# Holding the gathered rows' products and the weightings of reloaded tiles to TensorE's progress, two halves back

## The chip, the cores and the metric

One core of a Trainium2 chip runs one program. The metric is the device time of one execution in microseconds (us), lower is better. Engines: PE (TensorE, matmuls), DVE (VectorE), ACT (ScalarE), POOL (GpSimd), SP (SyncE, which issues most DMAs). Each works through its own queue in the order in which the program puts it there.

## What is computed

One layer of a two-branch model for 128 prompt tokens and 512 sample tokens: a mixer, then a layer of single-neuron experts (PEER). The change lies in the latter:

```python
s = jnp.einsum('chpd,hpnd->chpn', q, sub_keys)           # scores against 2 x 128 sub-keys per head
top_s, top_pos = lax.top_k(cand, PEER_TOPK)              # 16 experts of 16384 per head, 8 heads
g = jax.nn.softmax(top_s, axis=-1)
ue = jnp.take(peer_u, ids, axis=0)                       # rows of 2048 numbers
act = jax.nn.gelu(jnp.einsum('chkd,cd->chk', ue, xb))
ve = jnp.take(peer_v, ids, axis=0)
return jnp.einsum('chk,chkd->cd', g * act, ve)
```

Then x = LN2(ALPHA * x + gate2 * PEER(u)).

## The kernel before

PEER is computed in two ways at once. The 128 prompt tokens and the first 64 sample tokens are gathered: for each of their chosen experts an indirect DMA on POOL's queue (L825) brings 128 rows of 2048 numbers into a tile `rows`, 192 times from `peer_u` and 192 times from `peer_v`. A row tile of `peer_u` is multiplied by the tokens and summed in one DVE instruction (L858, `ustep`), one of `peer_v` is scaled and added to `gacc` in one (L869, `vstep`). These two are "products" below. There are three buffers for `rows`, four in the last stage.

The other 448 sample tokens go the dense way, through all 16384 experts. In the **S stage** PE computes scores `sps` of all experts, block by block (`s_half`, L934 to L936); ACT turns them into `ge` (L949), which is stored to DRAM (`ge_d`). Beside it a table of gates is built with small matmuls (L1024) and stored as `g_d`. In the **V stage** `ge` is loaded again (L1050) with its part of the table (`gt`, L1043), DVE multiplies them (L1061, the "weighting"), ACT rounds the product (L1063), DVE takes the rest (L1064), and PE multiplies with `peer_v` into `vps` (L88 to L90); DVE adds each `vps` to `vaccT` (L1139). `prep(e, ...)` issues the steps from L1050 to L1064 for expert block e, one block after each pair of halves in the V stage, and the first eight blocks in the S stage's last stretch.

The weights of both stages come 512 KB at a time into `wraw` (L82), which serves one **half**: 24 matmuls in the S stage as in the V stage. Each is split in two: ACT rounds it to `whi` (L76), DVE takes the rest, `wlo` (L77). Every third matmul of a half needs `wlo`. `wraw` has three buffers, and `whi` and `wlo` have three each as well, so the split for a half can be made only when PE has finished the half three before.

After each half the program notes its last matmul in `marks` and calls `pace`, which lets the gathers go on by `R_A` = 0.8 steps (by `r_v` in the V stage). One step of `gather_gen` issues a gather and, when as many are on the way as there are buffers, also the product of the oldest. The gather itself is tied to PE: `after(d, LAG)` makes it wait for the mark `LAG` = 2 halves back. `after` is this:

```python
def after(d, lag):
    if len(marks) > lag:
        tc.add_manual_dep(d.ins, marks[-1 - lag].ins.name, ...)
```

The order in each engine's queue is not the order in which the program is written: the framework that builds the program places instructions by its own estimate of when each can run, as far as their dependencies let it. A dependency on a mark is thus two things, a wait on the chip and a bound on how early the instruction can be placed.

Of the kernel before, what the change touches and what calls it, by code (L numbers as in the profile page):

```python
# [12 lines left out]
ALU = mybir.AluOpType  # L13
# [21 lines left out]
def layer_kernel(ctx: ExitStack, tc: tile.TileContext, i: dict, y_p: bass.AP, y_s: bass.AP, st_o: bass.AP):  # L35
# [786 lines left out]
    def gather_gen():  # L822
# [32 lines left out]

        def ustep(t, p, r):
            u, _, coef, dots, idx, gt_ = ctxs[t]
            V.scalar_tensor_tensor(r, r, 1.0, u, op0=ALU.mult, op1=ALU.mult, accum_out=dots[:, p:p + 1])  # L858
            if p % NBLK == NBLK - 1:
                sl = slice(p + 1 - NBLK, p + 1)  # L860
                S.activation(coef[:, sl], dots[:, sl], AF.Gelu_apprx_tanh)
                V.tensor_tensor(coef[:, sl], coef[:, sl], gt_[:, sl], op=ALU.mult)

        def vstep(t, p, r):
            _, acc, coef, _, idx, _ = ctxs[t]
            if p == 0:
                V.tensor_scalar(acc, r, coef[:, 0:1], None, op0=ALU.mult)
            else:
                V.scalar_tensor_tensor(acc, r, coef[:, p:p + 1], acc, op0=ALU.mult, op1=ALU.add)  # L869
            if t == 0 and p == 127:  # L870
                yield from close(acc, 0, 0, y_p[0])
            if t == 1 and p == 63:
                up = row_tile("up")
                Q.dma_start(up[0:NG2], acc[NG2:2 * NG2])
                yield
                acc = acc[0:NG2]
                V.tensor_tensor(acc, acc, up[0:NG2], op=ALU.add)
                yield from close(acc, 1, 128, y_s[0, 0:NG2])
# [29 lines left out]
    R_Q, R_A = 0.4, 0.8  # L908
    G_MOD, G_DVE = 4, 1
    gg = gather_gen()  # L910
    LAG = 2
    due, left = [0.0], [2 * (128 + 64) + 12]

    def pace(n):
# [116 lines left out]
    with ExitStack() as es:  # L1031
# [5 lines left out]
        gts_, loads, wts = {}, {}, {}  # L1037
# [14 lines left out]
        def prep(e, buf, x):  # L1052
            load_gt(e // 4)
            load_ge(e)
            if e % 4 == 0:
                load_gt(e // 4 + 1)
            for n in range(1, 4):
                load_ge(e + n)
            ge = loads[e]
            gev = ge.rearrange("p (b t) -> p b t", t=32)  # L1060
            V.tensor_tensor(gev, gev, gts_[e // 4][:, :, e % 4, :], op=ALU.mult)  # L1061
            eh, el = buf[:, x, :], buf[:, 8 + x, :]
            S.copy(eh, ge)  # L1063
            V.tensor_tensor(el, ge, eh.bitcast(F32), op=ALU.subtract)  # L1064
            wts[e] = (eh, el)
# [158 lines left out]
```

## Time and profile before

| what | us |
|---|---|
| three runs | 3967.94, 3979.97 (median), 3989.53 |
| the profiled execution | 3966.88 |
| its span, first to last instruction | 3964.8 |
| PE busy | 3768.2 |
| DVE busy | 3100.9 |
| DVE idle before products until rows landed, 1240 to 3934 us (140.4 + 135.8 + 45.6 + 32.5) | 354.3 |

The gathers and their products begin near 1240 us, the S stage's main stretch is 1470 to 2646 us, the V stage 2646 to 3934 us. Busy time of PE is the union of its matmuls, so what lacks to a stretch's length is time without a matmul. A line of the waits says which engine and line sat idle, until what was done, for how long in total, how often, and the longest. In the timelines the bracket at a row's end is the idle time of the engine just before it and what ended it. An idle engine costs only where PE ends up waiting for it.

### The profile page before, as it was taken

The numbers are of one execution on the slowest core, as the hardware profiler recorded it, in microseconds if no ns is written. First come the engines' busy times: TensorE is split into PE (matmuls) and PEld (weight loads), VectorE is DVE, ScalarE is ACT, GpSimd is POOL, SyncE is SP. The second block draws the span as 40 slices with busy tenths as digits, with TensorE's granted clock in tenths as the row PEclk, the third lists the DMA queues.
The fourth block names the chain that finished last, engine by engine and source line by source line (L and its number), as shares of the span: only waits on it lengthen the run. The fifth ranks groups of instructions, "written<-read, shape, count | busy, mean of one in ns | idle before, by whom it ended". The sixth has DMA issues, their size and how long they took to land.

```text
span 3964.8 us, 53756 instructions
## 1 busy us (share of the span) xinstructions
PE 3768.2 (95%) x20405; PEld 3357.2 (85%) x20405; DVE 3100.9 (78%) x4529; ACT 1595.3 (40%) x2707; POOL 721.1 (18%) x522
## 2 busy tenths in 40 slices
PE   7899899799999999999999999999999999999996
PEld 2688777678879989899898998888988899999896
DVE  5599965657899978788787887567887888888867
ACT  2111354533464347666666666223222222222221
POOL 0000111410000112222212222122222123322200
PEclk8899999999989999999999999999999999999998
DMA  9665444586444668898898898989998899999992
GB/s 363 209 204 179 154 138 163 170 257 233 155 144 166 209 236 303 288 326 319 292 325 292 305 325 290 326 307 334 336 332 322 322 332 329 339 330 347 321 241 80
DMA packets 408882, 1054.87 MB, mean 266 GB/s; under 512 B 27904, under 2 KB 253136, under 8 KB 355424
## 3 DMA queue, kind: packets, MB, share of 16 engines
q1 hardware_dynamic: 353328, 648.76, 49.2%
q0 software_dynamic: 55296, 402.68, 27.4%
q8 instruction: 160, 2.62, 0.3%
q14 instruction: 98, 0.80, 0.1%
HBM read 979.37 MB, written 71.38 MB: 265 GB/s over the span
## 4 chain that ended last, share of the span: by engine, by line
PE 61%; DMA 15%; DVE 13%; issue 6%; ACT 2%; POOL 2%; SPq 0%; DVEq 0%; POOLq 0%; ACTq 0%
PE vps L90 7%; PE vps L88 7%; PE vps L89 7%; PE sps L936 7%; PE sps L934 7%; PE sps L935 7%; DMA wa<-in_w_ada 3%; DVE wlo L77 3%; DMA rows<-in_peer_v,ids 3%; PE adab L156 2%; DMA gt<-g_d 2%; PE mm L258 2%; PE mm L256 2%; PE mm L89 2%; PE mm L90 2%
## 5 line engine op out<-in xcount | busy, mean ns | idle before, releaser
L76 ACT CAST whi<-wraw 128x1024 fp32r<-128x1024 f32 x704 | 737.5, 1049 | 1733.2 <-DMA wraw<-in_peer_v 346.2
L77 DVE TENSOR_TENSOR wlo<-wraw,whi 128x1024 fp32r<-128x1024 f32 x704 | 863.0, 1228 | 171.5 <-ACT whi L76 168.9
L934 PE MATMUL sps<-u2hi_a,whi 128*128 128x448 f32 x1760 | 648.9, 369 | 14.7 <-ACT ge L949 11.7
L936 PE MATMUL sps<-u2hi_a,wlo 128*128 128x448 f32 x1760 | 648.5, 368 | 6.5 <-DVE wlo L77 6.5
L935 PE MATMUL sps<-u2lo_a,whi 128*128 128x448 f32 x1760 | 647.9, 368 | 0.0
L869 DVE SCALAR_TENSOR_TENSOR gacc<-rows,coefs,gacc 128x2048 f32<-128x2048 f32 x190 | 446.3, 2349 | 186.5 <-DMA rows<-in_peer_v,ids 140.4
L858 DVE SCALAR_TENSOR_TENSOR rows<-rows,urow 128x2048 f32<-128x2048 f32 x192 | 439.2, 2288 | 168.7 <-DMA rows<-in_peer_u,ids 135.8
L90 PE MATMUL vps<-ehd,wlo 128*128 128x448 f32 x1024 | 377.3, 368 | 12.2 <-DVE wlo L77 12.2
L90 PE MATMUL vps<-ehl,wlo 128*128 128x448 f32 x1024 | 375.0, 366 | 8.9 <-DVE wlo L77 8.9
L89 PE MATMUL vps<-ehd,whi 128*128 128x448 f32 x1024 | 376.4, 368 | 0.0
L88 PE MATMUL vps<-ehd,whi 128*128 128x448 f32 x1024 | 376.3, 367 | 0.0
L88 PE MATMUL vps<-ehl,whi 128*128 128x448 f32 x1024 | 374.9, 366 | 0.0
L89 PE MATMUL vps<-ehl,whi 128*128 128x448 f32 x1024 | 374.3, 366 | 0.0
L934 PEld LDWEIGHTS sps<-u2hi_a,whi 128*128 128x128 f32 x1760 | 333.4, 189 | 42.9 <-ACT ge L949 12.2
L825 POOL DMA_INDIRECT rows<-in_peer_u,ids x128 | 189.8, 1483 | 983.8 <-PE gps L1024 287.0
L936 PEld LDWEIGHTS sps<-u2hi_a,wlo 128*128 128x128 f32 x1760 | 333.2, 189 | 37.5 <-DVE wlo L77 8.8
L935 PEld LDWEIGHTS sps<-u2lo_a,whi 128*128 128x128 f32 x1760 | 333.4, 189 | 26.9
L825 POOL DMA_INDIRECT rows<-in_peer_v,ids x128 | 193.3, 1510 | 514.8 <-PE gps L1024 140.1
L1020 ACT ACTIVATE A<-ab,gsp,nij 128x128 fp32r<-128x128 f32 x672 | 284.6, 487 | 1.6 <-DVE nij L1001 1.5
L332 DVE SCALAR_TENSOR_TENSOR ybuf<-z,par,ybuf 128x655 f32<-128x655 f32 x240 | 220.6, 921 | 6.4
L90 PEld LDWEIGHTS vps<-ehd,wlo 128*128 128x128 f32 x1024 | 192.9, 188 | 31.7 <-DVE wlo L77 14.5
L90 PEld LDWEIGHTS vps<-ehl,wlo 128*128 128x128 f32 x1024 | 192.2, 188 | 28.5 <-DVE wlo L77 12.5
(301 smaller groups left out, 7073.3 us busy)
## 6 DMA issues: line engine op xcount, KB each, us to landing
wraw<-in_peer_uT SPq DMA_DIRECT2D x256, 512.0 KB, 5.6
wraw<-in_peer_v SPq DMA_DIRECT2D x256, 512.0 KB, 6.1
wa<-in_w_ada SPq DMA_DIRECT2D x192, 512.0 KB, 4.1
wraw<-in_w_in SPq DMA_DIRECT2D x64, 512.0 KB, 4.7
wraw<-in_w_out SPq DMA_DIRECT2D x64, 512.0 KB, 6.0
wraw<-in_w_query SPq DMA_DIRECT2D x64, 512.0 KB, 3.5
ge_d<-ge SPq DMA_DIRECT2D x128, 224.0 KB, 5.2
g_d<-gst SPq DMA_DIRECT2D x14, 2048.0 KB, 13.4
```

The costliest lines, as they stand in the source:

```text
L76: S.copy(hi, raw)
L77: V.tensor_tensor(lo, raw, hi.bitcast(F32), op=ALU.subtract)
L88: T.matmul(out, ah, bh, start=first, stop=False)
L89: T.matmul(out, ah, bl, start=False, stop=False)
L90: return T.matmul(out, al, bh, start=False, stop=last)
L825: d = G.indirect_dma_start(out=r, out_offset=None, in_=src, in_offset=bass.IndirectOffsetOnAxis(ap=idx, axis=0))
L858: V.scalar_tensor_tensor(r, r, 1.0, u, op0=ALU.mult, op1=ALU.mult, accum_out=dots[:, p:p + 1])
L869: V.scalar_tensor_tensor(acc, r, coef[:, p:p + 1], acc, op0=ALU.mult, op1=ALU.add)
L934: T.matmul(sps, wh[:, kk, :], u2hi_a[:, k, :], start=(k == 0), stop=False)
L935: T.matmul(sps, wh[:, kk, :], u2lo_a[:, k, :], start=False, stop=False)
L936: mk = T.matmul(sps, wl[:, kk, :], u2hi_a[:, k, :], start=False, stop=(k == KT - 1))
L1020: S.activation(A[:, x], ab, AF.Relu, scale=nij[:, 1 + x, n:n + 1], bias=gsp[:, x, n:n + 1])
```

## The change

`after` gets a second use. The two products in `ustep` and `vstep` and the weighting in `prep` now also depend on the mark `PIN` = 2 halves back, counted when the instruction is written.

```diff
-            V.scalar_tensor_tensor(r, r, 1.0, u, op0=ALU.mult, op1=ALU.mult, accum_out=dots[:, p:p + 1])
+            after(V.scalar_tensor_tensor(r, r, 1.0, u, op0=ALU.mult, op1=ALU.mult, accum_out=dots[:, p:p + 1]), PIN)
...
-                V.tensor_scalar(acc, r, coef[:, 0:1], None, op0=ALU.mult)
+                after(V.tensor_scalar(acc, r, coef[:, 0:1], None, op0=ALU.mult), PIN)
             else:
-                V.scalar_tensor_tensor(acc, r, coef[:, p:p + 1], acc, op0=ALU.mult, op1=ALU.add)
+                after(V.scalar_tensor_tensor(acc, r, coef[:, p:p + 1], acc, op0=ALU.mult, op1=ALU.add), PIN)
...
-    LAG = 2
+    LAG, PIN = 2, 2
...
-            V.tensor_tensor(gev, gev, gts_[e // 4][:, :, e % 4, :], op=ALU.mult)
+            after(V.tensor_tensor(gev, gev, gts_[e // 4][:, :, e % 4, :], op=ALU.mult), PIN)
```

No arithmetic changes, but the order in the queues does. In DVE's queue in the S stage, the product of the gathered tile `rows_18253` stood before the change two rows behind `wlo_18292` and ahead of the splits that follow it (names in brackets are the semaphores waited for: DMASW of a gather, DMAHW of SP's DMAs, PE_49 of PE):

```order
L858 SCALAR_TENSOR_TENSOR rows_18253,dotss_10889<-rows_18253,urow_10890 128x2048 [waits DMASW2_49]
L1027 TENSOR_TENSOR gst_18122<-gps_18123,glo_18219 128x128x4 [waits Activation_49]
L77 TENSOR_TENSOR wlo_18325<-wraw_18322,whi_18324 128x1024 [waits DMAHW1_49,DVE_49]
L1010 TENSOR_TENSOR B_18451<-iota_69,ijgT_17400 128x512
L869 SCALAR_TENSOR_TENSOR gacc_10891<-rows_18319,coefs_10888,gacc_10891 128x2048 [waits DMASW3_49,DVE_49]
L1027 TENSOR_TENSOR gst_18122<-gps_18222,glo_18280 128x128x4 [waits Activation_49]
L77 TENSOR_TENSOR wlo_18388<-wraw_18385,whi_18387 128x1024 [waits DMAHW4_49]
```

In the changed program it stands here:

```order
L77 TENSOR_TENSOR wlo_18388<-wraw_18385,whi_18387 128x1024 [waits DMAHW4_49,Activation_49]
L1023 TENSOR_SCALAR A_18453<-iota_69,ijgT_17400,gsp_17402 128x128
L858 SCALAR_TENSOR_TENSOR rows_18253,dotss_10889<-rows_18253,urow_10890 128x2048 [waits DMASW2_49,PE_49]
L77 TENSOR_TENSOR wlo_18421<-wraw_18418,whi_18420 128x1024 [waits DMAHW5_49,DVE_49,Activation_49]
L869 SCALAR_TENSOR_TENSOR gacc_10891<-rows_18319,coefs_10888,gacc_10891 128x2048 [waits DMASW3_49,DVE_49,PE_49]
L1027 TENSOR_TENSOR gst_18122<-gps_18283,glo_18376 128x128x4 [waits Activation_49]
```

The product moved behind two more splits and waits for a mark as well as for its rows.

Near the end of the S stage, DVE's queue held the first weightings in a bunch, ahead of the split `wlo_23344`:

```order
L77 TENSOR_TENSOR wlo_23304<-wraw_23301,whi_23303 128x1024 [waits DMAHW6_49,PE_49,Activation_49]
L1061 TENSOR_TENSOR ge_23116<-ge_23116,gt_23114 128x448 [waits DMAHW7_49,DMAHW5_49,DMAHW0_49]
L1061 TENSOR_TENSOR ge_23189<-ge_23189,gt_23114 128x448 [waits DMAHW3_49]
L1061 TENSOR_TENSOR ge_23334<-ge_23334,gt_23114 128x448 [waits DMAHW2_49]
L869 SCALAR_TENSOR_TENSOR gacc_10891<-rows_23298,coefs_10888,gacc_10891 128x2048 [waits DMASW1_49,DVE_49]
L77 TENSOR_TENSOR wlo_23344<-wraw_23341,whi_23343 128x1024 [waits DVE_49,DMAHW7_49,PE_49,Activation_49]
```

In the changed program the first of them stands behind `wlo_23377`, and the next two splits further on, out of this piece:

```order
L77 TENSOR_TENSOR wlo_23304<-wraw_23301,whi_23303 128x1024 [waits DMAHW6_49,DVE_49,Activation_49]
L858 SCALAR_TENSOR_TENSOR rows_23256,dotss_10889<-rows_23256,urow_10890 128x2048 [waits DMASW0_49,PE_49]
L77 TENSOR_TENSOR wlo_23344<-wraw_23341,whi_23343 128x1024 [waits DMAHW7_49,DVE_49,Activation_49]
L869 SCALAR_TENSOR_TENSOR gacc_10891<-rows_23298,coefs_10888,gacc_10891 128x2048 [waits DMASW1_49,DVE_49,PE_49]
L77 TENSOR_TENSOR wlo_23377<-wraw_23374,whi_23376 128x1024 [waits DMAHW3_49,Activation_49]
L1061 TENSOR_TENSOR ge_23116<-ge_23116,gt_23114 128x448 [waits DMAHW5_49,DMAHW0_49,PE_49]
L77 TENSOR_TENSOR wlo_23417<-wraw_23414,whi_23416 128x1024 [waits DMAHW6_49,Activation_49]
```

Two splits have moved ahead of the first weighting, and the bunch is taken apart.

At 18 places, nearly all in the V stage, DVE's queue held three weightings in a row; one of them:

```order
L77 TENSOR_TENSOR wlo_28212<-wraw_28209,whi_28211 128x1024 [waits DMAHW1_49,Activation_49]
L1061 TENSOR_TENSOR ge_28202<-ge_28202,gt_28125 128x448 [waits DMAHW3_49]
L1061 TENSOR_TENSOR ge_28277<-ge_28277,gt_28125 128x448 [waits DMAHW2_49]
L1061 TENSOR_TENSOR ge_28349<-ge_28349,gt_28125 128x448 [waits DMAHW4_49]
L869 SCALAR_TENSOR_TENSOR gacc_26129<-rows_28197,coefs_10888,gacc_26129 128x2048 [waits DMASW3_49,DVE_49]
L77 TENSOR_TENSOR wlo_28245<-wraw_28242,whi_28244 128x1024 [waits DMAHW2_49,PE_49,Activation_49]
```

In the changed program each stands alone, the first of these five splits later:

```order
L1061 TENSOR_TENSOR ge_28202<-ge_28202,gt_28125 128x448 [waits DMAHW3_49]
L77 TENSOR_TENSOR wlo_28436<-wraw_28433,whi_28435 128x1024 [waits DMAHW7_49,Activation_49]
L1064 TENSOR_TENSOR ehd_23113<-ge_28202,ehd_23113 128x448 [waits Activation_49]
L858 SCALAR_TENSOR_TENSOR rows_28344,dotss_10889<-rows_28344,urow_26128 128x2048 [waits DMASW6_49,PE_49]
L77 TENSOR_TENSOR wlo_28469<-wraw_28466,whi_28468 128x1024 [waits DMAHW0_49,Activation_49]
```

The next weighting, of `ge_28277`, follows one split further on.

## Rows read from the trace of the kernel before

**Rows 1.** The page's first part: busy us of each engine, share of the span.

```profile
PE 3768.2 (95%) x20405; PEld 3357.2 (85%) x20405; DVE 3100.9 (78%) x4529; ACT 1595.3 (40%) x2707; POOL 721.1 (18%) x522
```

**Rows 2.** Stretches: start:end, length, busy PE, PEld, DVE, ACT, POOL; PEclk, DMA share, GB/s.

```profile
1470.00:2646.00 1176.00, 1145.77 (x5739) 1053.56 (x5740) 906.37 (x972) 705.73 (x1467) 260.27 (x176) 0.99 0.88 306
2646.00:3934.00 1288.00, 1266.81 (x6208) 1160.17 (x6208) 1031.96 (x1105) 336.99 (x397) 291.04 (x189) 1.00 0.89 311
```

**Rows 3.** Waits of PE, 1240 to 3934 us: total us, times, longest us.

```profile
PE vps L90 <- DVE wlo L77: 21.1, 15, 4.2
PE sps L934 <- ACT ge L949: 11.7, 2, 8.7
PE sps L936 <- DVE wlo L77: 6.5, 5, 2.4
PE gps L1024 <- ACT A L1020: 5.5, 5, 1.6
PE sps L934 <- ACT whi L76: 3.1, 2, 2.3
...
PE gps L1024 <- DVE A L1023: 2.2, 2, 1.5
```

**Rows 4.** Waits of DVE in the same stretch.

```profile
DVE gacc L869 <- DMA rows<-in_peer_v,ids: 140.4, 70, 9.4
DVE rows L858 <- DMA rows<-in_peer_u,ids: 135.8, 66, 8.5
DVE ge L1061 <- DMA gt<-g_d: 64.2, 23, 8.2
DVE gacc L869 <- DMA rows<-in_peer_v,id: 45.6, 28, 5.0
...
DVE rows L858 <- DMA rows<-in_peer_u,id: 32.5, 24, 4.9
...
DVE ge L1061 <- DMA ge<-ge_d: 21.7, 7, 4.8
```

**Rows 5.** Timelines of PE and of DVE, a stall in the V stage.

```profile
2985.31 0.36 PE L88 MATMUL vps<-ehd,whi 128*128 128x448 f32 x1
...
2985.92 0.36 PE L88 MATMUL vps<-ehd,whi 128*128 128x448 f32 x1
...
2989.12 0.47 PE L90 MATMUL vps<-ehd,wlo 128*128 128x448 f32 x1 [2.62 <-DVE wlo L77]
...
2986.77 0.62 DVE L1061 TENSOR_TENSOR ge<-ge,gt 128x448 f32<-128x448 f32 x1 [8.24 <-DMA gt<-g_d]
...
2987.84 1.22 DVE L77 TENSOR_TENSOR wlo<-wraw,whi 128x1024 fp32r<-128x1024 f32 x1
```

**Rows 6.** Timelines of DVE, ACT and PE, the longest stall, end of the S stage.

```profile
2521.36 1.16 DVE L1061 TENSOR_TENSOR ge<-ge,gt 128x448 f32<-128x448 f32 x2 [5.26 <-DMA gt<-g_d]
...
2522.02 0.56 ACT L1063 CAST ehd<-ge 128x448 fp32r<-128x448 f32 x1 [7.30 <-DVE ge L1061]
...
2529.61 0.54 ACT L949 ACTIVATE ge<-sps 128x448 f32<-128x448 f32 x1 [3.45 <-DVE ehd L1064]
...
2530.20 0.74 PE L934 MATMUL sps<-u2hi_a,whi 128*128 128x448 f32 x1 [8.72 <-ACT ge L949]
```

**Rows 7.** The tile `rows`: time to landing of its gathers; what POOL waited for.

```profile
DMA to landing us min/median/max: 5.2/8.3/15.7
...
POOL rows L825 <- PE vps L90: 635.0, 145, 15.4
```

**Rows 8.** The stretch around that stall, columns as in rows 2.

```profile
2505.00:2535.00 30.00, 21.28 (x97) 19.30 (x96) 14.66 (x17) 6.92 (x10) 2.81 (x3) 0.83 0.91 347
```

**Rows 9.** Timeline of ACT, a stall that begins with a late weight transfer.

```profile
2147.30 1.04 ACT L76 CAST whi<-wraw 128x1024 fp32r<-128x1024 f32 x1 [14.73 <-DMA wraw<-in_peer_uT]
```

**Rows 10.** DVE at the start of a gate block; ACT's waits for that start.

```profile
1613.93 2.35 DVE L869 SCALAR_TENSOR_TENSOR gacc<-rows,coefs,gacc 128x2048 f32<-128x2048 f32 x1 [4.94 <-DMA rows<-in_peer_v,ids]
...
ACT ab L1018 <- DVE nij L1000: 20.8, 4, 7.0
```

## Prediction

> **What bounds the kernel now.** I read the page first, then the stretches, then the waits of PE, then those of DVE, and last the timelines around single stalls. PE is busy for 95% of the span [rows 1], so what can be won is what PE lacks. The stretches show where: 30.2 us without a matmul in the S stage (1176 - 1145.8) and 21.2 us in the V stage (1288 - 1266.8), with DVE busy for 77% and 80% of them [rows 2]. The part from 1240 to 1470 us adds little. PE's waits [rows 3] name who was late: in the V stage nearly always `wlo` from DVE (21.1 us, 15 times), in the S stage ACT or DVE. The six rows come to 50.1 us.
>
> Why is `wlo` late on an engine that is idle a fifth of the time? DVE's own waits answer that [rows 4]: 354 us are spent before products until gathered rows land (four rows, 188 waits), 86 us before weightings until `gt` or `ge` lands. DVE works its queue in order, so every split behind such an instruction waits for a transfer that it does not need. The timeline shows it [rows 5]: DVE sat 8.24 us before a weighting until `gt` landed, the split ran only behind it, and PE stood 2.62 us. The longest stall has the same root [rows 6]: a weighting waited until 2521.36 us for `gt`; ACT, which had to round its result next, sat 7.30 us; the `ge` activation that frees PE's bank came behind that on ACT, and PE stood 8.72 us.
>
> **Sizes.** Three matmuls take 0.61 us [rows 5], so a half of 24 takes 4.9 us. A product takes 2.3 to 2.35 us [rows 10], a split 1.2, a weighting 0.6 [rows 5]. A gather lands 8.3 us after issue in the median, 15.7 at worst, and POOL mostly issues it when PE's mark comes [rows 7].
>
> **The products, part by part.** Count time from the end of the half g whose mark releases a gather. In the queue of before, counted over the whole program, 341 of 384 products stand behind the split for half g+3 and ahead of that for g+4. DVE is there soon after time 0 (that split needs only half g), and waits until 8.3; the product ends at 10.6, the split for g+4 at 11.8 or later. PE wants it about 15.1 (three halves and the first two matmuls). So there are 3.3 us of slack, gone when the gather takes 11.6 us or when a weighting stands in the same gap.
>
> In the changed queue the product stands behind the split for g+4 to g+7, most often g+5 (171) or g+6 (105), and its mark is always the half two before the last split ahead of it. For g+5 it may start at 14.7; the rows have landed, but for gathers of over 14.7 us. It ends at 17.0, the split for g+6 at 18.2, wanted at 24.9: 6.7 us of slack instead of 3.3. The new wait holds up that next split, which ACT and PE need. But this split could not run earlier anyway: with three buffers it needs the end of the same half. So the wait costs the product's 2.3 us at most, inside those 6.7 us. I cost it at nothing; the cover is DVE's lead of two halves, and if that is gone PE pays up to 2.3 us for each.
>
> How long a gather takes decides what the move is worth; measured are 8.3 us in the median [rows 7]. The Trainium skill's page DMA: Bandwidth & Descriptors, section Anatomy of one DMA, fits 2.0 us plus bytes over 436 GB/s to a DMA from GpSimd, which makes an estimate of 4.4 us for the 1 MB of rows. By it the old slack would be about twice what I count and moving the products would bring next to nothing; the trace does not agree, and the sum goes by the 8.3 us.
>
> **Weightings.** They move 5 to 11 splits later, and stand singly, where before up to four stood together. The wait for `gt` (64.2 us, at most 8.2 each [rows 4]) should nearly go, since a table now has five halves or more, over 24 us, beyond the time at which DVE stood waiting for it. Behind a weighting stand ACT's rounding and DVE's rest; both moved along with it. By the code the last block of a chunk still has about four halves before PE needs it. `ge` and `gt` loads on SP are issued later too, singly; the `wraw` loads behind them need splits of the same age, so I cost that at nothing. Its bound on the bad side is one late weight transfer as in [rows 9], some 3 us.
>
> **What goes.** By the rows of PE's waits [rows 3]:
> - V stage, 21.1 us: I take 17.5. A sixth stays, for stalls in which the weights themselves were late.
> - `sps` behind ACT's `ge`, 11.7 us in two waits: the 8.7 us one goes [rows 6]. The other, 3.0 us, begins with a weight transfer that ACT waited 14.7 us for [rows 9]; a product does not cause that, and it stays.
> - `sps` behind `wlo` and `whi`, 9.6 us: about half belongs to such late transfers; 4 go.
> - Gate matmuls behind ACT's or DVE's `A`, 7.7 us: they come at the start of a gate block, where ACT waits for `nij` (20.8 us in four waits), which stands behind a product that waits for rows [rows 10]. 5.5 go; in place of the rows such a product may now wait for a mark.
>
> Together 35.7 us of idle time. A stall also leaves PE slow: around the longest one, after PE had stood 8.7 us, the granted clock was 0.83 in the mean, so part of that stretch ran at 1.2 instead of 2.4 GHz; its 97 matmuls at 0.203 us would have taken 19.7 of the 30 us [rows 8], so 10.3 were lost where 8.7 were waited. By that ratio, 1.18, the 35.7 become 42.
>
> **What comes.** Near the change from the first gathered group to the second, three products, a weighting and the closing passes of the first group now stand between few splits. Nothing in the trace prices this order; its bounds are 0 (DVE's lead of two halves covers it) and the 8.7 us of the longest stall seen; I take 3, nearer to the many places where DVE's bunches cost PE 1 to 3 us [rows 3]. The waits themselves: the built program has 60 more separate ones on DVE, which no row prices; from 0 to the 0.62 us of a weighting each [rows 5] they are at most 37 us out of the 526 us that DVE idles in the two stages [rows 2], and I take 0.
>
> Sum: 42 - 3 = 39, so the profiled 3966.9 would become 3928. The median of the runs, 3980, is 13 above the profiled execution. What differs from run to run here is most likely when transfers land, so slower executions should hold more of these very stalls; I let the median fall further, by about 50, to **3930**.
>
> **Rivals.**
> - *The chip does what it did, in another order* (no change, 3960 to 3990). If the DMA engines, 0.88 and 0.89 busy [rows 2], set the pace, weights stay late and PE waits for `whi` or `wlo` all the same. For it: the 14.7 us [rows 9]. Against it: in the stall of [rows 5] the transfer that DVE waited for was not the one that PE needed. That the edit does nothing at all is excluded by the order, which moves.
> - *Only the weightings mattered* (no change, 3962). If gathers land early enough for most splits, as the 3.3 us of slack allow in the median, only stalls behind weightings go: the 8.7 us and, say, half of the 17.5, times 1.18, less 3, is 18, or 3949 for the profiled execution and 3962 by the median. The figure of the Trainium skill's page DMA: Bandwidth & Descriptors, Anatomy of one DMA, weighed above, would lead here. Against it: 188 waits for rows, up to 9.4 us [rows 4].
> - *DVE loses the time in which it worked ahead* (slower, about 4020). When weights come late, PE stands, no mark comes, and products that DVE used to run in the gap are held; they then run ahead of the split that PE waits for. It decides where a weight transfer is late by more than the slack of 6.7 us, and costs 2.3 us at each such place. If 35 places paid in full, 81 us less the 39 won make 42 more: 4009, by the median 4022. For it: ACT waits of 14.7 us do occur [rows 9]. Against it: only 20 waits for `wlo` are there in the two stages now [rows 3]. The Trainium skill's page TensorE: Matmul & The Clock Gate, table at its head, has VectorE's queue as strict first in, first out, which is what lets a held product block a split; the trace agrees that a wait holds what is behind it [rows 5].
>
> **How the numbers follow.** Forecast 0.77; no change by the first rival 0.09, by the second 0.06; slower 0.08. About 0.5%, 20 us, is what a measurement of this kernel can tell from no change, so faster means below 3960. The lower end: all 50 us of PE's waits with their 1.18 are 59, off the profiled execution 3908; a little luck more makes 3900. The upper end takes in the second rival and no change up to a little under the median: 3975. Below lie about 0.06, above about 0.13.
>
> **What would show it.** Right: DVE's waits for rows fall from 354 to under 120 us, those for `gt` from 64 to under 15; PE's waits for `wlo` in the V stage fall from 21 to under 6; no stall of over 4 us at the end of the S stage; products show short waits for PE. Wrong: POOL's gathers wait for DVE's products in place of PE's marks for over 200 us in all, DVE's idle time merely changes its name to PE, or PE's waits for `wlo` stay above 15 us.

## The result, and the profile after

The changed kernel takes 3923.6 us in the median, the kernel before beside it 3974.0: a ratio of 0.9868, with a 95% interval of 0.9825 to 0.9912. The forecast was 3930. Later runs of the changed kernel gave 3924.4 us and 0.9883 (0.9862 to 0.9905).

The profiled execution fell from a span of 3964.8 to 3912.0 us. The page's first part, after:

```profile
PE 3747.2 (96%) x20405; PEld 3347.7 (86%) x20405; DVE 3110.3 (80%) x4529; ACT 1597.2 (41%) x2707; POOL 946.3 (24%) x522
```

The work of PE, DVE and ACT is that of [rows 1]; POOL is busy 225 us longer with the same 522 instructions (see the last section). The two stretches after, S stage and V stage (columns as in [rows 2]):

```profile
1462.00:2610.00 1148.00, 1132.41 (x5738) 1045.84 (x5739) 902.12 (x967) 701.60 (x1467) 405.82 (x176) 0.99 0.90 314
2610.00:3880.00 1270.00, 1262.18 (x6203) 1160.05 (x6202) 1046.58 (x1109) 342.12 (x397) 370.57 (x189) 1.00 0.89 314
```

Against [rows 2] PE's time without a matmul falls from 30.2 to 15.6 us in the S stage and from 21.2 to 7.8 in the V stage, 28 us together. Its busy time, for the same matmuls but for six at the edges, falls by 13.4 and 4.6, another 18 us. So the two stages give 46 of the 52.8 us. Some 5 us more lie ahead of the first gather (it starts at 1236.9 instead of 1242.3 us), where both programs do the same work: that is what one execution differs from the next, for in the second profiles, below, it starts at 1240.6 in the changed kernel and at 1238.8 in the one before.

What PE waited for from 1240 us on, after (total us, times, longest; compare [rows 3]):

```profile
PE sps L934 <- ACT ge L949: 13.5, 1, 13.5
PE vps L90 <- DVE wlo L77: 6.9, 4, 5.4
...
PE gps L1024 <- ACT A L1020: 1.3, 1, 1.3
```

DVE's waits in the same stretch, after (compare [rows 4]):

```profile
DVE wlo L77 <- ACT whi L76: 129.5, 69, 8.1
DVE vaccT L1139 <- PE vps L90: 100.4, 97, 2.2
DVE rows L858 <- PE sps L936: 88.2, 51, 7.3
...
DVE gacc L869 <- DMA rows<-in_peer_v,ids: 20.5, 13, 2.4
...
DVE rows L858 <- DMA rows<-in_peer_u,ids: 12.7, 5, 3.6
...
DVE rows L858 <- DMA rows<-in_peer_u,id: 5.5, 1, 5.5
```

The 354 us before products until rows landed have become 39; no wait for `gt` or `ge` is left of 86. In their place DVE waits for PE's marks and for ACT. Its timeline in the S stage shows such a product, and that the split behind it is made at once:

```profile
2001.22 2.29 DVE L858 SCALAR_TENSOR_TENSOR rows<-rows,urow 128x2048 f32<-128x2048 f32 x1 [1.67 <-PE sps L936]
...
2004.44 1.22 DVE L77 TENSOR_TENSOR wlo<-wraw,whi 128x1024 fp32r<-128x1024 f32 x1
```

### The profile page after: what moved, and what is told of

Same layout as the page of the kernel before. It is cut to its first block, busy times and chain, and to the rows that moved or that the text cites. A ratio compares the mean times of both kernels' runs of the same rounds, so it can differ in the third digit from the quotient of the medians.

```text
span 3912.0 us, 53726 instructions
## 1 busy us (share of the span) xinstructions
PE 3747.2 (96%) x20405; PEld 3347.7 (86%) x20405; DVE 3110.3 (80%) x4529; ACT 1597.2 (41%) x2707; POOL 946.3 (24%) x522
## 4 chain that ended last, share of the span: by engine, by line
PE 78%; DVE 9%; DMA 8%; issue 2%; ACT 2%; POOL 1%; SPq 0%; DVEq 0%; POOLq 0%; ACTq 0%
PE vps L90 10%; PE vps L89 10%; PE vps L88 10%; PE sps L934 9%; PE sps L935 9%; PE sps L936 9%; DMA wa<-in_w_ada 4%; DVE wlo L77 2%; PE adab L156 2%; PE mm L89 2%; PE mm L90 2%; PE mm L88 2%; PE mm L258 2%; PE mm L256 2%; PE mm L254 2%
## 5 line engine op out<-in xcount | busy, mean ns | idle before, releaser
L934 PE MATMUL sps<-u2hi_a,whi 128*128 128x448 f32 x1760 | 644.9, 366 | 13.5 <-ACT ge L949 13.5
L858 DVE SCALAR_TENSOR_TENSOR rows<-rows,urow 128x2048 f32<-128x2048 f32 x192 | 439.0, 2287 | 132.4 <-PE sps L936 88.2
L869 DVE SCALAR_TENSOR_TENSOR gacc<-rows,coefs,gacc 128x2048 f32<-128x2048 f32 x190 | 446.1, 2348 | 75.2 <-PE sps L936 32.7
L825 POOL DMA_INDIRECT rows<-in_peer_u,ids x128 | 287.3, 2245 | 868.1 <-PE gps L1024 236.1
L825 POOL DMA_INDIRECT rows<-in_peer_v,ids x128 | 271.6, 2122 | 412.7 <-PE sps L936 83.5
L1139 DVE TENSOR_TENSOR vaccT<-vaccT,vps 128x448 f32<-128x448 f32 x240 | 145.9, 619 | 100.4 <-PE vps L90 100.4
## 6 DMA issues: line engine op xcount, KB each, us to landing
g_d<-gst SPq DMA_DIRECT2D x14, 2048.0 KB, 14.2
```

The costliest lines, as they stand in the source:

```text
L825: d = G.indirect_dma_start(out=r, out_offset=None, in_=src, in_offset=bass.IndirectOffsetOnAxis(ap=idx, axis=0))
L858: after(V.scalar_tensor_tensor(r, r, 1.0, u, op0=ALU.mult, op1=ALU.mult, accum_out=dots[:, p:p + 1]), PIN)
L869: after(V.scalar_tensor_tensor(acc, r, coef[:, p:p + 1], acc, op0=ALU.mult, op1=ALU.add), PIN)
L934: T.matmul(sps, wh[:, kk, :], u2hi_a[:, k, :], start=(k == 0), stop=False)
```

## The experiments

Below, "distance" is the median time from a gather's issue on POOL to the start of the product that reads its tile, found by pairing the two for every gather in the trace; "S" is the time from the S stage's first matmul to the V stage's first, "V" from there to the V stage's last; "rows" is DVE's whole wait for gathered rows, "weights" is ACT's wait for `wraw` in the V stage. Stages and waits are of the one profiled execution, ratios of all runs.

| kernel | distance S / V | rows | S | V | weights | ratio to before |
|---|---|---|---|---|---|---|
| before | 9.1 / 9.3 | 354 | 1175.0 | 1286.8 | 339 | 1 |
| before, second profile | 9.2 / 9.2 | 368 | 1181.0 | 1298.2 | 300 | |
| changed | 13.6 / 19.2 | 39 | 1148.0 | 1269.9 | 120 | 0.9868 |
| changed, second profile | 14.0 / 19.3 | 37 | 1155.7 | 1271.5 | 114 | 0.9883 |
| e1: products alone | 14.2 / 19.3 | 46 | 1152.6 | 1275.0 | 134 | 0.9878 |
| e2: weightings alone | 9.1 / 8.6 | 387 | 1172.5 | 1264.3 | 118 | 0.9913 |
| e3: order, no wait | 12.0 / 17.1 | 51 | 1146.8 | 1273.8 | 131 | 0.9874 |
| e5: gathers two halves later | 9.1 / 9.9 | 345 | 1166.5 | 1275.6 | 205 | 0.9968 |
| e10: gathers one half later | 10.1 / 14.4 | 184 | 1159.8 | 1271.7 | 131 | 0.9896 |
| e8: three halves back | 10.2 / 14.4 | 158 | 1163.4 | 1265.4 | 44 | 0.9890 |
| e6: products in S only | 13.5 / 8.8 | 205 | 1153.2 | 1265.9 | 128 | 0.9880 |
| e4: table loads later | 13.7 / 19.2 | 35 | 1151.9 | 1268.2 | 142 | 0.9887 |
| e7: room at the end of S | 14.1 / 19.2 | 31 | 1141.0 | 1269.1 | 132 | 0.9878 |
| e11: e6 and e7 together | 13.9 / 9.0 | 199 | 1142.8 | 1266.6 | 181 | 0.9845 |

The second profiles say how far a stage may be read: the same kernel differs by 6 to 8 us in S, and by 2 to 11 us in V.

**One part at a time.** e1 leaves the weightings as before, e2 the products.

```diff
# e1
-            after(V.tensor_tensor(gev, gev, gts_[e // 4][:, :, e % 4, :], op=ALU.mult), PIN)
+            V.tensor_tensor(gev, gev, gts_[e // 4][:, :, e % 4, :], op=ALU.mult)
# e2, the same for the three products
-            after(V.scalar_tensor_tensor(r, r, 1.0, u, ...), PIN)
+            V.scalar_tensor_tensor(r, r, 1.0, u, ...)
```

> Only the products wait for the mark two halves back, the weightings do not. Theory: most of the gain (52.8 us between the two profiled spans) comes from what DVE held while it waited for gathered rows (354 us of waits); products alone give a ratio to the kernel before of about 0.992 (30 us off), DVE's waits for rows fall under 60 us, its waits for gt stay near 64 us, and the V stage keeps PE waits for wlo of 8 to 15 us behind weightings. Rival, only the weightings mattered: ratio 0.998 or more.

> Only the weightings wait for the mark, the products do not. Theory: about 20 us off, ratio 0.995; DVE's waits for gt nearly vanish, those for rows stay at 300 us or more, PE's waits for wlo in the V stage about halve. Rival, only the weightings mattered: the whole gain, ratio 0.987. If the two parts add, e1 and e2 together give 0.987.

Measured: 3922.4 us, 0.9878 (0.9864 to 0.9892) for the products alone; 3939.4 us, 0.9913 (0.9896 to 0.9930) for the weightings alone. The two do not add: 1.2% and 0.9% give 1.3% together. By stage they differ. The S stage is short with the products held and, within the spread, as long as before without; the V stage is short with either. Here are the waits of e2 from 1240 us on, DVE's and then PE's:

```profile
DVE rows L858 <- DMA rows<-in_peer_u,ids: 147.5, 76, 8.6
DVE gacc L869 <- DMA rows<-in_peer_v,ids: 138.0, 68, 6.9
DVE rows L858 <- DMA rows<-in_peer_u,id: 51.5, 32, 3.4
DVE gacc L869 <- DMA rows<-in_peer_v,id: 49.8, 32, 3.7
...
PE sps L934 <- ACT ge L949: 16.5, 2, 12.0
...
PE vps L90 <- DVE wlo L77: 2.5, 3, 1.1
```

387 us of waits for rows, more than before, and yet PE's waits for `wlo` in the V stage fall from 21.1 to 2.5 us. So in the V stage products that wait for rows cost next to nothing in e2, as the 3.3 us of slack have it. In e1 it is the other way round: DVE still waits 49.2 us for `gt` and 26.6 for `ge`, products hardly wait, and `wlo` costs PE 9.6 us. That the two hurt only where they meet in one gap fits both runs, but no run shows it gap by gap. PE's waits in e1:

```profile
PE vps L90 <- DVE wlo L77: 9.6, 3, 5.1
PE sps L934 <- ACT ge L949: 5.8, 1, 5.8
```

ACT's waits for weights in the V stage tell what follows from the pair. Before and after:

```profile
ACT whi L76 <- DMA wraw<-in_peer_v: 339.2, 90, 8.1
```

```profile
ACT whi L76 <- DMA wraw<-in_peer_v: 120.4, 32, 12.3
```

A weight load is issued when DVE's split has freed `wraw`. With either part of the change the late loads fall to 118 to 134 us, so they were late because DVE was, and not because the transfers set the pace.

**The order without the wait.** Products and weightings stand where the change puts them (in the trace all but one of the 512 follow the same number of splits as in the changed kernel), but they wait for no mark on the chip.

```diff
-def after(d, lag):
+def after(d, lag, cls=mybir.DependencyClass.Sync):
-  mybir.DependencyInfo(mybir.DependencyClass.Sync, ...)
+  mybir.DependencyInfo(cls, ...)
# the four places of the change
-after(..., PIN)
+after(..., PIN, mybir.DependencyClass.NoSync)
```

> The same marks hold products and weightings in the order in which the queues are filled, but no wait on the chip goes with them. Products stand behind as many splits as in the changed kernel (171 of 384 behind the one for five halves after the gather's mark). Theory: the gain is the order's and the wait on the chip costs and brings nothing, since the split behind it needs the same half: ratio 0.987 within 0.4%. Rival, the wait itself does it, by keeping gathers, products and loads in step with PE: ratio near 1. Other rival, the wait costs DVE time in which it could work ahead: ratio under 0.983.

Measured: 3922.8 us, 0.9874 (0.9859 to 0.9889). This cannot be told from the changed kernel. What the change brings is the places in the queue; the wait as such brings and costs nothing that can be measured.

**Only the distance, undone.** If the S stage gains because rows have landed before DVE comes to them, gathers that start later must give the gain back though every product keeps its tie.

```diff
-    LAG, PIN = 2, 2
+    LAG, PIN = 0, 2      # e5; e10: 1, 2
```

> The changed kernel with the gathers tied to the last mark instead of the mark two halves back. Each gather is issued two halves (9.8 us) later, while the products keep their ties, so 260 of the 384 products again stand behind the split of the third half after the gather's mark, as in the kernel before (there 341), instead of the fifth or sixth; the weightings stay where the change puts them. Theory (the S stage gains because the product starts 14.7 us instead of 9.4 us after its gather's mark, with rows that take 8.8 to 9.9 us): DVE waits for rows again, over 200 us in all, and the S stage goes back from 1148 to 1165-1175 us; the V stage stays at 1262-1274 because its gain belongs to the weightings; time 3935-3948. Rival (the gain comes from where the products stand among the splits, evenly behind marks, and not from their distance to the gather): S stage 1145-1153, time 3917-3928 whatever the waits for rows are.

> The changed kernel with the gathers tied to the mark one half back instead of two, so that the distance from gather to product lies between the changed kernel's and that of the run with the gathers two halves later. Theory (distance is what the S stage gains by; rows need 9 to 10 us and sometimes 13): the product starts about 9.8 us after the gather's mark, just where half the rows have landed, so DVE waits for rows 100-200 us in all and the S stage is 1152-1162, time 10-15 us above the changed kernel beside it. Rival (9.8 us is enough, since the rows' median is below it): S stage and time as the changed kernel's, within 4 us.

Measured for e5: 3948.9 us, 0.9968 (0.9955 to 0.9981), so three quarters of the gain are gone. DVE's waits:

```profile
DVE gacc L869 <- DMA rows<-in_peer_v,ids: 145.3, 67, 5.5
DVE rows L858 <- DMA rows<-in_peer_u,ids: 116.4, 59, 6.4
```

With two smaller rows for the second group (46.3 and 36.9) the waits for rows are back at 345 us, the distance in the S stage is 9.1 us as before, and the stage is 1166.5 us long. The products kept their places: 296 of the 384 follow the same number of splits as in the changed kernel, 88 one more. So the rival, that the places among the splits matter and not the distance, falls. The time lies just above the theory's range (3935 to 3948). The profiled execution, 3939.9 us, is the fastest of the twelve, so its stages (V 1275.6, a little longer than in the changed kernel) show somewhat less than the median lost. e10, one half later, lies between in distance, waits and S stage, as the theory has it, but its S stage is only 4 us longer than in the second profile of the changed kernel, within the spread, and its time of 3928.9 only 4.5 us above the changed kernel beside it, where 10 to 15 were expected; the intervals overlap. The rival had said within 4. So a distance of 10 us gives most of the gain; whether 14 us gives more, these runs cannot tell.

**One half more.** Ties three halves back move the products earlier in DVE's order.

```diff
-    LAG, PIN = 2, 2
+    LAG, PIN = 2, 3
```

> The changed kernel with products and weightings tied to the mark three halves back instead of two. The products then stand behind the split of the third to sixth half after the gather's mark (88, 132, 114, 45 of them) instead of mostly the fifth and sixth, and the ties come one half earlier in DVE's order. Theory (distance to the gather is what counts, and about 9 us is needed): about a quarter of the products wait for rows again, 40-120 us in all, the S stage is between the two kernels, 1150-1160, time 3922-3932. Rival (any tie to a mark does it): S 1145-1150, time 3918-3925.

Measured: 3920.1 us, 0.9890 (0.9873 to 0.9907). The waits for rows, 158 us, and the S stage of 1163.4 go beyond what the theory expected, in its direction; the median is the rival's, and cannot be told from the changed kernel's (the profile is of the slowest of its five runs, 3929.3 us). Alone it decides nothing; distance, waits and S stage are those of e10.

Down the table's first columns, S goes with the distance: 9.1 us and 1166 to 1181, 10.1 us and 1160 to 1163, 12 to 14 us and 1147 to 1156 (leaving out e7 and e11, where the end of the stage is changed). The ends of this row are further apart than two profiles of one kernel; neighbours in it are not.

**The end of the S stage.** There the largest stall should have gone, and it grew to 13.5 us. The timelines of ACT and PE, after:

```profile
2479.90 1.05 ACT L76 CAST whi<-wraw 128x1024 fp32r<-128x1024 f32 x1 [8.60 <-DMA wraw<-in_peer_uT]
...
2492.31 1.04 ACT L76 CAST whi<-wraw 128x1024 fp32r<-128x1024 f32 x1 [8.87 <-DMA wraw<-in_peer_uT]
2498.19 1.04 ACT L76 CAST whi<-wraw 128x1024 fp32r<-128x1024 f32 x1 [4.83 <-DMA wraw<-in_peer_uT]
2499.14 0.56 ACT L1063 CAST ehd<-ge 128x448 fp32r<-128x448 f32 x1
2501.06 0.54 ACT L949 ACTIVATE ge<-sps 128x448 f32<-128x448 f32 x1 [1.36 <-DVE ehd L1064]
...
2501.66 0.74 PE L934 MATMUL sps<-u2hi_a,whi 128*128 128x448 f32 x1 [13.47 <-ACT ge L949]
```

No weighting waits for `gt` here any more; the weights are late three times. The chain of waits of that stretch (start, us, what; a length is that of the transfer), and what SP waited for between 2440 and 2540 us:

```profile
2461.74 14.39 DMA g_d<-gst
...
2476.57 12.29 DMA ge_d<-ge
...
2489.77 8.32 DMA wraw<-in_peer_uT
```

```profile
SPq L1050 <- DMA ge_d<-ge: 10.6, 1, 10.6
SPq L82 <- DVE coefs L862: 10.0, 1, 10.0
...
SPq L1043 <- DMA g_d<-gst: 3.0, 1, 3.0
```

SP's waits show its queue held by what stands first in it. It had issued weights at 2462.87 and, after 10.0 us until a `wraw` was free, at 2472.78; it stood 3.0 us until the last 2 MB of the gate table were stored, since the load of the table's first part (L1043) came next, and issued weights again at 2477.77. Then it stood 10.6 us until a tile of `ge` was stored that it was to load again (L1050), and only at 2489.77 issued the weights of the cast at 2498.19. Taken in order, the weights of the casts at 2479.90 and 2492.31 are those issued at 2462.87 and 2477.77: they took 17.0 and 14.5 us to their casts, which SP's waits do not explain. The DMA engines were full then (window 2478 to 2494 us, columns as in [rows 2]):

```profile
2478.00:2494.00 16.00, 10.19 (x51) 9.16 (x49) 7.54 (x6) 3.15 (x3) 2.11 (x2) 0.91 1.02 416
```

But PE did not wait for weights: it waited for the `ge` activation that frees one of its two banks (`ps_s`). The block of scores for it was finished at 2478.5 us, and it ran at 2501.06, 22.5 us later. Its own wait names DVE's L1064, the rest of the first reloaded tile. By the code the `ge` tiles that go out and most of those that come back share three buffers (`gep`), and this activation needs one that the first reloaded tile holds until its weighting, rounding and rest are done. DVE's timeline, after:

```profile
2494.53 0.62 DVE L1061 TENSOR_TENSOR ge<-ge,gt 128x448 f32<-128x448 f32 x1
...
2500.41 0.62 DVE L1064 TENSOR_TENSOR ehd<-ge,ehd 128x448 fp32r<-128x448 f32 x1
```

The table had landed at 2487.1 us. But the weighting stood behind the split of the weights that were cast at 2492.31, and its rounding behind the cast at 2498.19: it is there that the late weights come in. Before, the weighting ran as soon as `gt` landed [rows 6]. In all fourteen profiles this activation follows within 0.2 us upon that rest, and in thirteen of them PE's stall is the activation's delay less 9.1 us (9.8 in e5), in which PE works on in its other bank: 17.8 and 8.7 us in the kernel before, 22.5 and 13.5 after. In e1, where the weightings are not tied, SP stands 10.2 us before the same load, and yet the delay is 14.8 us and the stall 5.8. In the nine profiles with tied weightings and the end of the stage as it was, the stall is 10.1 to 15.8 us. So it is the weightings' new place that made it grow.

First attempt: the table's loads are issued six halves after the store, and pinned there.

```diff
-                if g > 1:
-                    after(d, 1)
+                after(d, 1)
...
-                if n == 0:
+                if n == 6:
                     load_gt(0)
```

> The changed kernel, with the loads of the first two gt tables moved six halves later, away from the last 2 MB store of the gate table; they also wait for a mark. The changed kernel still has one stall of 13.5 us at the end of the S stage, where the DMA engines are at 415 GB/s and SP's queue stands. Theory: transfers crowd there, not DVE's order, and they are what ended the stall of 8.7 us of the kernel before as well: the stall falls under 4 us and the ratio to the kernel before is about 0.984. Rival, the weighting's place sets that stall: it stays over 8 us and the ratio is 0.987.

Measured: 3926.4 us, 0.9887 (0.9873 to 0.9902), and a stall of 12.7 us at the same place. The table itself now came too late for the first weighting, and with it for the activation (DVE's timeline):

```profile
2505.05 0.62 DVE L1060 TENSOR_TENSOR ge<-ge,gt 128x448 f32<-128x448 f32 x1 [6.67 <-DMA gt<-g_d]
```

Second attempt: the gate work ends eight halves sooner, so that there is room between it and the weightings.

```diff
-        S_LATE = 28
+        S_LATE, ROOM = 36, 8
...
-        for n in range(S_LATE):
-            if n % 2 == 0:
+        for n in range(-ROOM, S_LATE - ROOM):
+            if n >= 0 and n % 2 == 0:
```

> The changed kernel with the last gate block's store 8 halves (39 us) earlier, S_LATE 36 instead of 28, and the table, tile loads and the eight weightings of the S stage where they were, counted from the stage's end. Theory (the 13.5 us stall at the end of the S stage is crowding: the last 2 MB store, the stored tiles and the table loads run beside the weights, and the weight tiles come late): with 39 us between the store and the table loads the stall falls below 5 us, the waits of ACT for weights there from 22 us in three to below 8, S stage 1136-1143, time 3910-3918. Rival (the loads of table and tiles alone crowd the weights out, with or without the store): the stall stays at 10-14 us, time 3920-3928; and if the gate work, pressed into 8 halves less, loses as much on ACT's A matrices as the stall gives back, the S stage is 1146-1155 with the stall gone.

Measured: 3915.3 us, 0.9878 (0.9859 to 0.9897), and an S stage of 1141.0 us, the shortest so far and as the theory has it. The stall of 13.5 us became two waits:

```profile
PE sps L934 <- ACT ge L949: 5.3, 2, 3.3
```

SP's queue in that run shows that the edit did it otherwise than I had written: store and table loads stayed together and moved forward together.

```profile
2427.77 0.53 SPq L1029 DMA_DIRECT2D g_d<-gst  x1
...
2442.11 0.32 SPq L1043 DMA_DIRECT2D gt<-g_d  x1
```

The load of the table still comes 14 us behind the store, but over 30 us sooner, and no wait of 10 us for a stored tile follows it. PE ran through that stretch (window 2440 to 2460 us, with the DMA engines just as full):

```profile
2440.00:2460.00 20.00, 20.00 (x100) 18.57 (x100) 10.50 (x7) 3.60 (x4) 2.65 (x3) 1.00 1.03 419
```

ACT's waits for weights there did not fall below 8 us, as expected: the three longest are 9.5, 4.1 and 8.4 us, as much together as the three after (8.6, 8.9, 4.8). But no activation needs a reloaded tile's buffer there, and PE waits 2.0 us (ACT's and PE's timelines, e7):

```profile
2464.34 1.04 ACT L76 CAST whi<-wraw 128x1024 fp32r<-128x1024 f32 x1 [8.39 <-DMA wraw<-in_peer_uT]
2465.29 0.54 ACT L949 ACTIVATE ge<-sps 128x448 f32<-128x448 f32 x1
...
2465.88 0.48 PE L934 MATMUL sps<-u2hi_a,whi 128*128 128x448 f32 x1 [1.96 <-ACT ge L949]
```

So neither full DMA engines nor 22 us of late weights stop PE for long by themselves. The other wait, 3.3 us, is that for the first reloaded tile: its table load had been issued 53 us before, but its weighting waited at last for its mark, and the activation came 12.4 us after its block. So the theory gave the right time, but the crowding that it named is still there; what went is the meeting of late weights and a weighting that the activation needs. No run lets the weightings of the S stage alone go free, nor gives the reloaded tiles buffers of their own.

**Products held in the S stage only.** By e2 a product that waits for rows in the V stage is harmless, and holding it is not free: at the change of groups near 3120 us the changed kernel has a stall that e2 has not. DVE's, ACT's and PE's timelines, after:

```profile
3121.05 2.29 DVE L858 SCALAR_TENSOR_TENSOR rows<-rows,urow 128x2048 f32<-128x2048 f32 x1 [5.49 <-DMA rows<-in_peer_u,id]
...
3124.98 1.05 ACT L76 CAST whi<-wraw 128x1024 fp32r<-128x1024 f32 x1 [12.33 <-DMA wraw<-in_peer_v]
...
3129.07 1.11 PE L90 MATMUL vps<-ehd,wlo 128*128 128x448 f32 x2 [5.36 <-DVE wlo L77]
```

```diff
+    def hold(d):
+        if not more:          # `more` is filled when the V stage begins
+            after(d, PIN)
# the three products
-after(..., PIN)
+hold(...)
```

> The changed kernel with the products tied to marks in the S stage only; in the V stage the products stand where the scheduler puts them, and the weightings stay tied in both. Theory (the S gain is the products', the V gain the weightings'; products tied in the V stage bring nothing there): S stage 1145-1153, V stage 1262-1268 as in the run with the weightings alone, waits of DVE for rows about 100-200 us, all in the V stage, time 3912-3922, a ratio to the kernel before of 0.984-0.988. Rival (the parts add in the V stage too, so it loses there when the products are let go): V stage 1272-1280, time 3925-3932.

Measured: 3917.8 us, 0.9880 (0.9860 to 0.9899): the time in the expected range, the V stage at 1265.9 us as in e2, the S stage within its spread. Against the changed kernel this is not decided. Most of the 205 us of waits for rows lie in the V stage, 39 do not. The stall of 5.4 us at the change of groups is gone: PE's waits for `wlo` in the V stage are 3.0 us in two, 1.9 at the longest.

**Both together, and the changed kernel beside it.** e9 is the changed kernel again, e11 has the edits of e6 and e7.

> The changed kernel again, so that the next two stand beside it on one chip. Both theories expect a ratio of 0.985-0.989 to the kernel before, S stage 1146-1153, V stage 1265-1275, and again one stall of TensorE of 10-15 us near the end of the S stage.

> Both edits that looked good apart: the last gate block's store 8 halves earlier, and the products tied in the S stage only. If they add: S stage 1138-1146, V stage 1262-1268, time 10-14 us below the changed kernel beside it, ratio to the kernel before 0.982-0.985. Rival (what is saved at the end of the S stage comes back at the group change of the V stage or in the gate work): within 5 us of the changed kernel, ratio 0.986-0.989.

The changed kernel's S stage came out 3 us above what was expected, its stall at 13.7 us as expected. Measured on one chip: 3924.4 us for e9 (3916.8 to 3929.9, six runs) and 3908.6 for e11 (3903.7 to 3912.9, five runs), a ratio to the kernel before of 0.9845 (0.9823 to 0.9867). No run of the one reaches into the other; e11 is 15.9 us faster than the changed kernel, a little more than the 10 to 14 expected. Its ratio lies below those of e6 and e7, taken on another chip, but the intervals overlap; by the stages most of the gain is the end of S (1142.8 against 1155.7), and that of V (1266.6 against 1271.5) is within the spread. PE's waits from 1240 us on, e11 (its lines stand four further down):

```profile
PE sps L938 <- ACT ge L953: 5.1, 2, 3.3
...
PE vps L90 <- DVE wlo L77: 1.6, 2, 1.0
```

Last, a second profile of the kernel before.

> The kernel before again, for a second profile: how far S and V stage differ between two executions of one kernel. If the gains of the stages are real, S stage 1170-1180 and V stage 1280-1290, DVE's waits for rows 330-380 us; if the stages trade time from one execution to the next, one of them is off by over 8 us.

Measured: S 1181.0, V 1298.2 us, a time of 3980.4. Both stages are above what was expected and V is 11 us longer than in the first profile, the sign that had been named for a stage that cannot be trusted; but both grew, so they did not trade. The waits for rows, 368 us, lie within. So before and changed kernel differ by 19 to 33 us in S and by 15 to 28 in V, which is what the gains of single stages are good for.

## Why the prediction was right, point by point

- **What bounds the kernel.** Right: PE lacked matmuls because DVE stood before transfers that the split behind did not need. e2 and e5 put the waits for rows back (387 and 345 us), and most of the S stage's time with them (1172.5 and 1166.5). In the V stage they did not (1264.3 and 1275.6).
- **The products.** Right, to the microsecond: from the mark of its gather to the product's start the S stage now has 14.7 us in the median, as worked out for g+5, and rows land 8.8 us after the mark before and 9.9 after the change. The rival that only the weightings matter falls with e1, where the products alone bring a gain that cannot be told from the whole. But the slack argument was used for both stages, and holds as a price only in the S stage. In the V stage the slack of 3.3 us sufficed in e2, and the stage became short by either part.
- **The weightings.** Their waits for tables, 64.2 us in [rows 4], went as said (for what their new place cost, see the next point). Alone they bring the V stage's whole gain (e2) and nothing in the S stage.
- **What goes: the 8.7 us stall** [rows 6]. Wrong. The chain was read rightly, from the weighting over the rounding to the activation. But the place of the weighting was priced by when PE needs its block, four halves later, and not by when the activation needs its buffer: moving it behind more splits took away its wait for `gt` and made it later all the same. The stall became 13.5 us in one execution and 13.7 in the other, and 5.8 in e1 without the tie.
- **The other terms.** V stage: 17.5 of 21.1 us were to go; 1.5 stayed, besides 5.4 at the change of groups, which the sum has under what comes. S stage behind `wlo` and `whi`: 4 of 9.6 were to go and over 9 went, in the second profile 5. Gate matmuls: 5.5 of 7.7 expected, 6.4 measured.
- **What comes.** The change of groups was put at 3 us; it is 5.4 us in the one stall (the bounds were 0 and 8.7) and the reason given, products between few splits, is the one that the timeline shows. Without the products' ties in the V stage it goes (e6, e11).
- **The clock's share.** 28 us of idle time went, where 35.7 - 3 = 32.7 were counted, and 18 us of busy time on top, where the factor 1.18 gave 6; between the second profiles it is 30 and 22. I had sized it at the longest stall; the many short ones cost more. In the two stages, matmuls that start 300 to 420 ns after the one before them, some 0.1 to 0.2 us over the usual 0.203, fell from 95 to 21, which is 11 us (the granted clock at those of before is 0.61 in the mean in the S stage and 0.81 in the V stage). Starts under 300 ns apart give under 2 us, and the rest lies at the ends of the stalls themselves. The errors cancel in part: too much idle time, too little for the clock.
- **From the profiled execution to the median.** The sum gave 39 us for the profiled execution, which fell by 53 (3966.9 to 3913.8). For the median 11 more were added, since slower executions should hold more of these stalls; it fell by 50 (3974.0 to 3923.6), and by 41 in the later runs (3965.5 to 3924.4). The second profile of before, 13.5 us slower than the first, does hold some 7 us more time without a matmul in the two stages, so the reason has something for it. But the sum was too small for the profile, and the addition made it up: that 3930 came within 7 us is in part luck.
- **The waits at nothing.** Right: e3 has the order without the waits, and the same time.
- **What would show it.** Waits for rows under 120 (39), for `gt` under 15 (0) and waits of products for PE (88.2 us in 51 and 32.7 in 25 in the S stage) came true; `wlo` under 6 just not (6.9), no stall over 4 us at the end of the S stage not. One sign of failure seems to show: POOL's gathers wait for DVE. The waits of POOL, after:

```profile
POOL rows L825 <- DVE vaccT L1139: 238.9, 74, 8.9
...
POOL rows L825 <- DVE rows L858: 55.7, 10, 7.3
```

The row with `vaccT` names an instruction that a gather does not need; it is the last event before. Timed one by one, the gathers are issued 0.27 us after their mark in the median, before and after the change in both stages. Only the 55.7 us and 22.3 more, of L869, name a product.

## What to carry to other kernels

An instruction that waits for a transfer in an in-order queue is to stand where the transfer has landed: here 9 us after the issue left 354 us of waits for gathers of 9, 10 us gave most of the gain and 14 us all of it. Where it stands decides, not whether it also waits for a mark. Where several kinds of instruction wait in one queue, take away one kind at a time before dividing the gain: here one part alone brought 1.2%, the other 0.9%, and both together 1.3%. And before an instruction is moved back, ask who waits for what it frees, not only for what it makes: here an activation needed the buffer of the tile that the weighting reads, and the stall that was to go grew by 5 us.

## What the runs showed of the hardware

The issue of a gather on POOL takes longer when DVE is in the middle of a product. For the first group its median is 2.87 us (rows of `peer_u`) and 2.17 (`peer_v`) after, and 1.26 and 1.13 before; the shortest is 0.94 in all four. Two timelines of after, DVE's and POOL's, show both cases:

```profile
3399.98 2.34 DVE L869 SCALAR_TENSOR_TENSOR gacc<-rows,coefs,gacc 128x2048 f32<-128x2048 f32 x1
...
3404.14 1.23 DVE L1139 TENSOR_TENSOR vaccT<-vaccT,vps 128x448 f32<-128x448 f32 x2 [0.68 <-PE vps L90]
...
3400.12 3.02 POOL L825 DMA_INDIRECT rows<-in_peer_u,id  x1 [3.93 <-DVE ehd L1064]
3404.98 0.94 POOL L825 DMA_INDIRECT rows<-in_peer_v,id  x1 [1.84 <-DVE vaccT L1139]
```

The first starts 0.14 us into a product, which reads two tiles of SBUF, and ends 0.82 us after it; the second runs beside `vaccT`, which reads one input from PSUM, and takes its usual 0.94. Sorted by what DVE did at the start, 195 gathers of after that began during a product took 2.9 to 3.1 us in the mean, 75 beside L1139 0.94, 27 beside an idle DVE 0.94. Before, 167 gathers began during a product as well, but mostly later in it: they took 1.9 us in the mean. The change ties gather and product to marks that come at the same moment, so they start together. The Trainium skill's page SBUF — State Buffer, section SBUF: two separate sides, says that VectorE with two SBUF inputs and a GpSimd operation that reads SBUF share a port pair, which the one that starts first holds to its end. The trace agrees: the gather's issue ends only after the product. Landing came a microsecond later in the S stage (8.8 to 9.9 us from the mark), which the distance covers; how much of it is this is not shown, for gathers that began beside an idle DVE landed later there too (8.2 to 9.0 us after their issue).
